# Side-by-side transfers in the ordering clock of a hybrid encoder-trunk kernel

## The chip, the cores and the metric

The kernel runs on one core of a Trainium2 chip. The metric is the device time of one execution in microseconds (us); several executions are timed, and one more is profiled.

## The reference

One layer of an encoder trunk on 2048 tokens of 1024 channels, all in float32. The part that matters here is branch C:

```python
h = rmsnorm(x, pre_g) * (1 + scale) + shift          # shift, scale, gate from silu(c) @ w_ada
q_lat, kv_lat, k_rope, gm_in, rw_in, z, g_logit = split_last(h @ w_in, IN_SPLITS)
y_mla = mla_mixer(...)      # attention of 8 heads, causal by chunks of 64
y_gm  = gmlp_mixer(...)     # gated mixing inside 128-token blocks
# branch C, rwkv7_mixer, 8 heads of 64, one step per token:
#   state = state * w_t + (state @ a_t) b_t^T + v_t k_t^T ;  y_t = state @ r_t
branches = stack([y_mla, y_gm, y_rw]) * silu(z)
merged = sum over branches of (branch @ w_br) * sigmoid(g_logit)
x = x + gate * rmsnorm(merged @ w_out, post_g)
```

## The kernel before, in words

**Stages.** The 2048 tokens are worked in four blocks of 512. For each block `s` there is a recurrence stage, `wkv(s)` (L969), and then an attention stage, `attention(s)` (L1334); the last block ends with `finish` (L1660). Every large product is made of three matmuls with 128x512 results (`mm3`, L595), since each operand is split into a high and a low part; they write the PSUM tiles `pd` and are called gemm matmuls below. Their weights (`wh`, `wl`) are loaded again for every use, by transfers that SP issues. Gemm work that nothing in a stage needs soon (gates, branch projections, the end of the block before) is the filler of that stage.

**A round of the recurrence.** Branch C is computed in chunks, two heads at a time, so a stage has four rounds and the kernel sixteen. A round goes through these steps:

- `prepare` (L1009): TensorE multiplies `ard` with `bk` (the `pst<-ard,bk` matmuls). ScalarE copies parts of the result to `abc`; VectorE makes the masked copies `ak` and `MB`.
- At the end of `prepare`, four transfers write quarters of `abc` side by side into the DRAM tile `md`, and four read `md` into quarters of `mb`.
- `inverses` (L1148): VectorE inverts small triangular matrices in 31 steps. They are 58 short instructions that write `X` and `tx`, each needing the one before. Then four transfers write `X` into quarters of the DRAM tile `xd`.
- `advance` (L1171): four transfers read `xd` into diagonal blocks of `xtb`. TensorE's first use of them are the `pss<-Pm,xtb` matmuls. Then follow `u`, `n`, `Wm`, `UV` and `QG`.
- `states` (L1236): eight small steps in turn on TensorE (`pss<-S,QG`) and VectorE (`S<-pss`), and the output `Y`.

**What sets the order.** The program is written by generators that take turns. A class `Pace` (from L99) keeps a clock for this. After each instruction is written, `note` (L154) puts down when it would end: it takes the latest of the times at which its inputs were written and its outputs last used (`wrote`, `used`, by tile name), finds a free slot on its engine, and adds a duration from a formula. For a transfer these are 0.45 us of the queue, 1.1 us, its bytes, and 0.8 us (`DLAT`). `ready` (L260) asks of each generator when the tiles of its next TensorE step would be there, and `run` (L291) lets the one go on that is ready first; filler goes where nothing else is ready.

TensorE runs its instructions in the order in which the program writes them (L331). The orders of VectorE, ScalarE, GpSimd and of SP's transfers are made by the framework's scheduler from the same program. On every engine, and on SP's queue, an instruction whose input isn't there holds up all that stand behind it. The clock itself isn't run on the chip: it decides orders alone.

Helpers issue every instruction through one traced call, so all rows of the profile carry its line, L123, and are told apart by their tiles.

Of the kernel before, what the change touches and what calls it, by code (L numbers as in the profile page):

```python
# [92 lines left out]
class Pace:  # L93
# [60 lines left out]
    def note(self, i):  # L154
        eng = str(i.engine).split(".")[-1]
        dma = "DMA" in type(i).__name__
        src, dst, n, full, f32 = [], [], 1, 0, False
        for l, aps in ((src, i.ins), (dst, i.outs)):
            for a in aps:
                ap = getattr(a, "bass_ap", None)  # L160
                if ap is None:
                    continue
                l.append(ap.tensor.name)
                m = 1
                for _, c in a.ap[1:]:
                    m *= c
                full += l is src and m > 1
                if dma:
                    m = 4 * m * a.ap[0][1]
                if eng != "PE" or l is dst:  # L170
                    n = max(n, m)
                elif a.dtype == F32:
                    f32 = True
        dep = 0.0
        for x in src:
            dep = max(dep, self.after(self.wrote.get(x), eng))
        for x in dst:
            for e in self.used.get(x, {}).items():
                dep = max(dep, self.after(e, eng))
        if eng == "PE":  # L180
            if f32 and not i.is_transpose:
                dur = 2 * max(.111, n * 2 / 2400)
            elif f32:
                dur = max(.108, n * 2 / 2400)
            else:
                dur = max(.061, n / 2400 + .0135)
            (r, c), (nr, nc) = i.tile_position, i.tile_size
            if dep <= self.t and all(r >= b or r + nr <= a for a, b in self.beside[1]):

                at = self.beside[0]  # L190
                self.beside[1].append((r, r + nr))
            else:
                at = max(self.t, dep)
                self.beside = at, [(r, r + nr)]
            t, p = max(self.t, at + dur), self.t
            self.pe += t - max(p, at)
            self.t = t
        elif dma:
            dur = n / 3.6e5
            t = self.slot("queue", max(dep, self.t - self.early), .45) + 1.1  # L200
            t = self.slot("DMA", t, dur) + dur + DLAT
            eng = "DMA"
        else:
            psum = any(x.startswith(("pd", "ps")) for x in src)
            op = type(i).__name__
            if eng == "Activation":
                f = str(i.func).split(".")[-1]
                if f in ("Exp", "Gelu", "Sin") and f != self.table or f == "Tanh" and self.table not in ("Exp", "Gelu"):
                    self.table = "Exp" if f == "Tanh" else f
                    t = self.slot(eng, max(dep, self.t - self.early), 1.28)  # L210
                dur = .08 + n * .00084 + .04 * (not psum) + .09 * (len(src) > 1) + .09 * (len(dst) > 1)
            elif eng == "DVE":
                dur = .065 + n / (960 if psum or full > 1 or n < 128 else 1920) + .065 * (full < len(src))
                if "Reciprocal" in op:
                    dur = .07 + n * .0063
                elif "Scan" in op or "Reduce" in op:
                    dur = n * (.0021 if "Scan" in op else .00118)
            else:
                dur = .12 + n * .00216 if n <= 512 else .55 + n * .0013
                if n <= 16 and "TensorTensor" in op:  # L220
                    dur = .3 + n * .165
            dur *= SLOW

            port = ("port",) if eng == "Pool" or eng == "DVE" and not psum else ()
            t = self.slot(eng, max(dep, self.t - self.early), dur, port) + dur
        for x in dst:
            self.wrote[x] = (eng, t)
        for x in src + dst:
            u = self.used.setdefault(x, {})
            u[eng] = max(u.get(eng, 0.0), t)  # L230
# [1539 lines left out]
```

## Time and profile before

| | us |
|---|---|
| median of 3 runs | 3145.57 |
| lowest and highest run | 3144.99, 3150.43 |
| the profiled execution | 3146.36 |
| its span, first to last instruction | 3144.4 |
| TensorE matmuls (PE), busy | 2927.0 |
| VectorE (DVE), busy | 1731.6 |
| ScalarE (ACT), busy | 1216.7 |
| GpSimd (POOL), busy | 621.5 |
| TensorE's mean granted clock, as a share of full speed | 0.964 |

The profiled execution takes 3146.36 us, 1.96 us more than its span. Busy times are sums over the span; PE is TensorE's matmuls, PEld its weight loads beside them, SPq the sequencer of SyncE that issues transfers. The clock is granted at one of two levels, 1.00 (2.4 GHz) or 0.50 (1.2 GHz). Moved bytes come to 654.17 MB, 208 GB/s on average.

### The profile page before, as it was taken

To read this page: it belongs to the slowest core of one execution; us is meant where nothing else is said; L and a number is where in the kernel's file an instruction comes from. 1 tells how busy PE (TensorE), PEld (TensorE's weight loads), DVE (VectorE), ACT (ScalarE), POOL (GpSimd) and SP (SyncE) were. 2 spreads that over 40 slices of the span, in tenths; PEclk is the share of its full clock that TensorE was granted. 3 is DMA by queue.
4 is the path that set the end of the run, shared out by engine and by line. 5 is a ranking of instruction groups with operands and counts; after the bars stand their busy time and mean duration, and the time that the engine had idled before them with its cause. 6 is when DMAs were issued, how large, how long until landed. Compare 5 with 4: busy or idle time off the path is not lost. (4 is left out here: it accounts for less than half of the span.)

```text
span 3144.4 us, 47954 instructions
## 1 busy us (share of the span) xinstructions
PE 2927.0 (93%) x16156; PEld 2391.6 (76%) x16156; DVE 1731.6 (55%) x4578; ACT 1216.7 (39%) x2806; POOL 621.5 (20%) x618
## 2 busy tenths in 40 slices
PE   5889998789999999999999998999999999999997
PEld 4667776668867787878877776887787777788876
DVE  6434767365366654466356664446645665566632
ACT  4324433353333424444232323544433232466621
POOL 2223232241022212122011101113201110222210
PEclk8999999879999999999999998999999999999998
DMA  8888855767566678765676577556558657744366
GB/s 273 271 271 264 251 182 182 242 210 229 200 210 223 192 226 265 225 196 166 211 251 199 166 230 231 185 177 209 155 169 250 198 171 230 224 137 128 113 207 204
DMA packets 524962, 654.17 MB, mean 208 GB/s; under 512 B 141648, under 2 KB 254380, under 8 KB 524716
## 3 DMA queue, kind: packets, MB, share of 16 engines
q1 hardware_dynamic: 524544, 651.06, 65.9%
q8 instruction: 128, 2.10, 0.3%
q14 instruction: 118, 0.97, 0.1%
q10 hardware_dynamic: 172, 0.05, 0.0%
HBM read 461.91 MB, written 189.01 MB: 207 GB/s over the span
## 5 line engine op out<-in xcount | busy, mean ns | idle before, releaser
L123 PE MATMUL pd<-hh,wh 128*128 128x512 f32 x1952 | 814.5, 417 | 19.3 <-ACT wh L123 10.3
L123 PE MATMUL pd<-hh,wl 128*128 128x512 f32 x1952 | 776.2, 398 | 6.1 <-DVE wl L123 4.3
L123 PE MATMUL pd<-hl,wh 128*128 128x512 f32 x1952 | 774.6, 397 | 2.5 <-DVE hl L123 1.5
L123 PEld LDWEIGHTS pd<-hh,wh 128*128 128x128 f32 x1952 | 374.5, 192 | 102.9 <-ACT wh L123 13.2
L123 PEld LDWEIGHTS pd<-hh,wl 128*128 128x128 f32 x1952 | 372.9, 191 | 94.7 <-DVE wl L123 8.3
L123 PEld LDWEIGHTS pd<-hl,wh 128*128 128x128 f32 x1952 | 374.8, 192 | 70.2 <-DVE hl L123 3.4
L123 DVE TENSOR_TENSOR pw<-pst,ph 128x512 fp32r<-128x512 f32 (+2 forms) x352 | 197.0, 568 | 255.2 <-ACT ph L123 253.6
L123 PE MATMUL pd<-brh,wh 128*128 128x512 f32 x576 | 252.0, 438 | 23.0 <-DVE gt L123 13.6
L123 ACT ACTIVATE ph<-pst 128x512 fp32r<-128x512 f32 (+2 forms) x352 | 171.7, 497 | 235.8 <-PE pst L123 197.8
L123 PE MATMUL pd<-brl,wh 128*128 128x512 f32 x576 | 232.4, 404 | 1.3 <-DVE brl L123 1.3
L123 PE MATMUL pd<-brh,wl 128*128 128x512 f32 x576 | 232.4, 403 | 0.0
L123 DVE TENSOR_SCALAR_CACHE_REDUCE p<-pss 128x512 f32<-128x512 f32 (+2 forms) x320 | 192.6, 607 | 62.6 <-PE pss L123 58.7
L123 ACT ACTIVATE p<-p,nm 128x512 f32<-128x512 f32 (+3 forms) x288 | 189.8, 661 | 79.1 <-DVE nm L123 78.9
L123 POOL TENSOR_TENSOR wl<-wr,wh 128x512 fp32r<-128x512 f32 x96 | 129.2, 1347 | 442.1 <-ACT wh L123 362.9
L123 ACT ACTIVATE wh<-wr 128x512 fp32r<-128x512 f32 x162 | 101.5, 628 | 220.0 <-PE pd L123 75.7
L123 PE MATMUL pst<-consts,p 128*128 128x128 f32 x1088 | 165.2, 277 | 7.9 <-DVE otm L123 3.1
L123 PEld LDWEIGHTS pd<-brh,wh 128*128 128x128 f32 x576 | 112.3, 195 | 58.6 <-DVE gt L123 11.6
L123 PE MATMUL pso<-ph,v 128*128 128x256 f32 x576 | 153.5, 287 | 2.4 <-ACT ph L123 2.3
L123 PE MATMUL pso<-pw,v 128*128 128x256 f32 x576 | 149.2, 286 | 6.3 <-DVE pw L123 6.0
L123 PEld LDWEIGHTS pst<-consts,p 128*128 128x128 f32 x1088 | 130.4, 143 | 24.7 <-issue 6.5
L123 PE MATMUL pss<-kh,qh 96*128 96x512 f32 (+2 forms) x320 | 131.1, 410 | 18.8 <-ACT kh L123 18.1
L123 POOL TENSOR_TENSOR kl<-stg,kh 96x512 fp32r<-96x512 f32 x80 | 103.8, 1300 | 223.8 <-ACT kh L123 194.6
(291 smaller groups left out, 4947.5 us busy)
## 6 DMA issues: line engine op xcount, KB each, us to landing
wh<-kept SPq DMA_DIRECT2D x486, 256.0 KB
wl<-kept SPq DMA_DIRECT2D x486, 256.0 KB
kept<-wh SPq DMA_DIRECT2D x162, 256.0 KB
kept<-wl SPq DMA_DIRECT2D x162, 256.0 KB
wr<-in_w_in SPq DMA_DIRECT2D x120, 256.0 KB
gate_d<-gt SPq DMA_DIRECT2D x64, 256.0 KB
part_d<-gt SPq DMA_DIRECT2D x64, 256.0 KB
p<-part_d SPq DMA_DIRECT2D x64, 256.0 KB
```

Source lines behind the costliest of these rows:

```text
L123: r = f(*a, **k)
```

## The change

The clock's rule for transfers is altered in two lines. Before, a transfer into a tile waited, in the clock, for every earlier use of that tile, earlier transfers into or out of it too; four transfers into quarters of one tile were timed one after the other. After, a transfer no longer waits in the clock for other transfers that use the tile it writes, and a tile counts as written when the latest of its transfers has landed. Nothing else is altered; no instruction, size or buffer is.

```diff
@@ -176,7 +176,8 @@
             dep = max(dep, self.after(self.wrote.get(x), eng))
         for x in dst:
             for e in self.used.get(x, {}).items():
-                dep = max(dep, self.after(e, eng))
+                if not (dma and e[0] == "DMA"):
+                    dep = max(dep, self.after(e, eng))
@@ -224,7 +225,8 @@
         for x in dst:
-            self.wrote[x] = (eng, t)
+
+            self.wrote[x] = (eng, max(t, self.wrote[x][1]) if dma and x in self.wrote else t)
```

The programs have the same 14129 matmuls and 2911 transfers, in other orders. Three places of the third recurrence stage, first round (chunks of block 2, heads 0 and 1), show what moved. A line of "..." stands where rows are left out.

TensorE at the first use of `xtb`, before: between the second half of the next round's `pst<-ard,bk` and `xtb` stand the rest of that round's `prepare` and 51 gemm matmuls.

```order
L123 MATMUL pst<-ard,bk 128x128 x8
L123 MATMUL pso<-vt,ak 64x64 x4
...
L123 MATMUL pst<-consts,bkb 128x128 x8
...
L123 MATMUL pst<-r,rkb 128x512
...
L123 MATMUL pss<-Pm,xtb 128x128 x8
L123 MATMUL pd<-hh,wh 128x512
L123 MATMUL pd<-hl,wh 128x512
L123 MATMUL pd<-hh,wl 128x512
```

The same place now:

```order
L123 MATMUL pst<-consts,sq 128x2 x4
L123 MATMUL pd<-brh,wh 128x512
L123 MATMUL pd<-brl,wh 128x512
L123 MATMUL pd<-brh,wl 128x512
...
L123 MATMUL pss<-Pm,xtb 128x128 x8
L123 MATMUL pst<-consts,sq 128x128 x4
L123 MATMUL pst<-consts,ard 128x128 x4
```

`xtb` is now used while the next round's `prepare` is still at its `sq` products, which stand on either side; its `ard,bk` and `bkb` matmuls follow later. Up to that round's second `pst<-lat,w2a` matmul the two orders are equal; from there to `sq` there are 24 gemm matmuls now, and were 12.

VectorE at the last steps of `inverses`, before (`ak` and `MB` are of the next round):

```order
L123 TENSOR_TENSOR ak<-pst,consts 128x256
L123 TENSOR_TENSOR tx<-X,mb 128x24
L123 TENSOR_TENSOR MB<-pst,consts 128x2x2x64
L123 TENSOR_TENSOR X<-X,tx 128x8x3
L123 TENSOR_TENSOR ak<-pst,consts 128x256
L123 TENSOR_TENSOR tx<-X,mb 128x16
L123 TENSOR_TENSOR MB<-pst,consts 128x2x128
L123 TENSOR_TENSOR X<-X,tx 128x8x2
L123 TENSOR_TENSOR tx<-X,mb 128x8
L123 TENSOR_TENSOR X<-X,tx 128x8
```

Now:

```order
L123 TENSOR_TENSOR tx<-X,mb 128x28
L123 TENSOR_TENSOR X<-X,tx 128x7x4
L123 TENSOR_TENSOR tx<-X,mb 128x24
L123 TENSOR_TENSOR X<-X,tx 128x8x3
L123 TENSOR_TENSOR tx<-X,mb 128x16
L123 TENSOR_TENSOR X<-X,tx 128x8x2
L123 TENSOR_TENSOR tx<-X,mb 128x8
L123 TENSOR_TENSOR X<-X,tx 128x8
```

The next round's masks no longer stand among these steps. Between the first and the last `X` of this round there were 29 other instructions, and there are 20 now.

SP's queue around the transfers of `X`, before:

```order
L123 DMA wl<-kept 128x512
L123 DMA xd<-X 256x1x32 x4
L123 DMA wh<-kept 128x512
L123 DMA gt<-gate_d_373 128x512
L123 DMA wl<-kept 128x512
L123 DMA xtb<-xd 32x8x32 x4
L123 DMA mg_d_352<-gt 128x512
```

Now:

```order
L123 DMA wh<-kept 128x512
L123 DMA gt<-gate_d_373 128x512
L123 DMA xd<-X 256x1x32 x4
L123 DMA xtb<-xd 32x8x32 x4
L123 DMA X<-in_consts 128x256
L123 DMA wl<-kept 128x512
```

The three loads that stood between `xd` and `xtb` stand elsewhere; the next weights follow `xtb`.

Counted on TensorE between the last `pst<-ard,bk` matmul of a round and its first `pss<-Pm,xtb` matmul, gemm matmuls and others (the latter in brackets):

| stage | before, rounds 1 to 4 | now, rounds 1 to 4 |
|---|---|---|
| 1 | 318 (80), 309 (111), 183 (132), 237 (97) | 216 (47), 138 (95), 114 (63), 126 (57) |
| 2 | 216 (80), 210 (107), 177 (139), 165 (125) | 129 (27), 126 (63), 141 (63), 141 (57) |
| 3 | 210 (80), 201 (103), 174 (106), 174 (129) | 120 (27), 132 (71), 108 (75), 126 (39) |
| 4 | 210 (80), 201 (103), 186 (105), 180 (129) | 120 (27), 132 (71), 108 (75), 126 (39) |

## Rows read from the trace of the kernel before

**Rows 1.** The page, part 1: busy us, share of the span, instructions of each engine.

```profile
PE 2927.0 (93%) x16156; PEld 2391.6 (76%) x16156; DVE 1731.6 (55%) x4578; ACT 1216.7 (39%) x2806; POOL 621.5 (20%) x618
```

**Rows 2.** TensorE's waits over the span: who waited for what, us, times, longest.

```profile
PE pss L123 <- DMA xtb<-xd: 2.0, 1, 2.0
```

**Rows 3.** TensorE in time, third stage, round 1: start, us, operation, count.

```profile
1607.08 1.16 PE L123 MATMUL pst<-ard,bk 64*128 64x128 f32 x16
...
1635.72 0.95 PE L123 MATMUL pst<-consts,sq 128*128 128x2 f32 x8
...
1670.67 1.95 PE L123 MATMUL pss<-Pm,xtb 128*128 128x128 f32 x16
```

**Rows 4.** VectorE in time, the same round: first and last `X`.

```profile
1628.03 0.25 DVE L123 SCALAR_TENSOR_TENSOR X<-mb,X 128x31 f32<-128x31 f32 x1
...
1654.80 0.17 DVE L123 TENSOR_TENSOR X<-X,tx 128x8 f32<-128x8 f32 x1
```

**Rows 5.** SP's queue in time, the same round: when its transfers were issued.

```profile
1655.00 2.57 SPq L123 DMA_DIRECT2D xd<-X  x4
...
1659.38 1.81 SPq L123 DMA_DIRECT2D xtb<-xd  x4
```

**Rows 6.** The chain that ended last: start, us, what.

```profile
2358.72 23.14 PE pd L123 x102
...
2451.26 4.01 DMA wl<-kept
...
2657.74 1.79 DMA xtb<-xd
```

**Rows 7.** One stretch of that round: us, then each engine's busy time (count).

```profile
1627.00:1656.00 29.00, 27.50 (x163) 21.43 (x161) 27.21 (x90) 7.20 (x15) 4.17 (x3) 1.00 0.72 236
```

**Rows 8.** The same stretch, VectorE's instructions on `X` and `tx` alone.

```profile
1627.00:1656.00 29.00, 14.80 (x58) 1.00 0.72 236
```

**Rows 9.** Twelve stretches, stages 1 to 3: last `ard,bk` to first `xtb` matmul.

```profile
283.50:377.50 94.00, 88.84 (x453) 68.79 (x452) 66.88 (x186) 43.18 (x86) 25.03 (x20) 0.98 0.83 248
337.40:432.90 95.50, 93.02 (x513) 74.26 (x513) 61.65 (x151) 38.77 (x73) 25.97 (x22) 1.00 0.84 252
442.30:520.50 78.20, 68.62 (x416) 54.00 (x417) 52.61 (x147) 27.92 (x66) 21.88 (x19) 0.96 0.50 152
503.70:580.90 77.20, 72.95 (x420) 59.04 (x420) 41.03 (x115) 22.84 (x48) 20.20 (x19) 1.00 0.72 226
885.40:958.30 72.90, 67.19 (x351) 52.08 (x350) 41.57 (x110) 22.04 (x54) 16.48 (x14) 0.93 0.71 216
943.30:1017.30 74.00, 71.22 (x410) 55.51 (x409) 49.04 (x139) 24.06 (x49) 15.08 (x14) 1.00 0.68 215
1028.80:1101.20 72.40, 66.03 (x416) 50.72 (x417) 45.77 (x138) 29.40 (x77) 16.73 (x16) 0.95 0.59 181
1094.70:1161.20 66.50, 63.15 (x376) 51.22 (x377) 38.81 (x119) 22.43 (x84) 11.15 (x12) 0.93 0.67 206
1608.20:1670.70 62.50, 61.01 (x345) 47.91 (x344) 38.67 (x111) 16.98 (x45) 7.86 (x7) 1.00 0.78 236
1655.80:1728.20 72.40, 68.95 (x396) 54.50 (x397) 46.15 (x134) 19.29 (x41) 8.70 (x9) 0.98 0.64 196
1745.50:1808.60 63.10, 59.75 (x347) 44.97 (x345) 39.70 (x123) 25.25 (x70) 10.16 (x11) 0.97 0.62 188
1800.30:1865.90 65.60, 62.55 (x390) 49.85 (x390) 39.52 (x121) 22.28 (x90) 7.52 (x9) 1.00 0.72 214
```

**Rows 10.** Two stretches where attention begins in stage 2; the granted clock is third from last.

```profile
1215.60:1220.60 5.00, 0.01 (x1) 0.01 (x1) 1.38 (x2) 2.96 (x6) 0.93 (x1) 1.00 0.76 179
1220.60:1227.40 6.80, 5.97 (x15) 4.50 (x16) 1.95 (x5) 2.88 (x6) 4.20 (x5) 0.50 0.64 206
```

**Rows 11.** Sum over 283:616, 885:1200, 1608:1914 and 2400:2700, the four recurrence stretches.

```profile
sum 1254.00, PE 1189.54 PEld 946.37 DVE 783.71 ACT 398.39 POOL 229.04; mean PE 297.38 PEld 236.59 DVE 195.93 ACT 99.60 POOL 57.26
```

## The prediction

> **What bounds the kernel now.** Read part 1 of the page first: TensorE's matmuls are busy for 2927.0 of 3144.4 us, VectorE for 1731.6 [rows 1]. So TensorE's own order, and what it waits for in that order, sets the time. The change alters no instruction, only orders, and the order of TensorE is the one that it alters directly. Next, TensorE's waits: of all its waits one single wait, of 2.0 us, was for `xtb` [rows 2]. In fifteen of sixteen rounds the inverted matrices were there before TensorE came to them. That cover is what the change takes away, so the question is how thick it was.
>
> Then one round in time. In stage 3, round 1, the last `ard,bk` matmul ends at 1607.08 + 1.16 = 1608.24, and TensorE comes to `xtb` at 1670.67 [rows 3]. In between, `X` runs on VectorE from 1628.03 to 1654.97 [rows 4], the four `xd` stores are issued from 1655.00 and the four `xtb` loads from 1659.38 to 1661.19 [rows 5]. A landing takes 1.79 us after the last issue, as the one `xtb` wait in the chain shows [rows 6]. So `xtb` lands at 1662.98. The **need** of this round is 1662.98 - 1608.24 = 54.7 us, TensorE gave it 62.4, and 7.7 us were to spare.
>
> Where do 54.7 us go? Transfers are the small part: from the last `X` to the landing it is 8.0 us for eight of them. In the stretch 1627 to 1656 VectorE is busy for 27.21 of 29.00 us [rows 7], and only 14.80 of that is `X` and `tx` [rows 8]. The other 32 instructions take 12.4 us, 0.39 each. The inversion shares VectorE with everything else.
>
> **The change, part by part.** Before, the clock timed four transfers into quarters of a tile in a row, which its own formula makes more than 2.35 us each; a round has four such groups, so some 25 us of its forecast were waiting that the queue doesn't do (rows 5 show four issued in 1.81 us). This error stood in for another: the clock fills gaps on VectorE freely, while the real engine runs its order. The change removes the first error and leaves the second.
>
> *TensorE comes earlier.* A gemm matmul costs 23.14 / 102 = 0.227 us [rows 6]. In stage 3, round 1, the order is unchanged up to the second `lat,w2a`; 12 more gemm matmuls then stand ahead of `sq`, which started at 1635.72 [rows 3]: 1635.72 + 2.7 + 0.95 for `sq` + 6 x 0.227 = 1640.7. That is 30 us sooner than 1670.67. Of these, 90 gemm matmuls (210 less 120) make 20.4 us, and 53 others 9.6, or 0.18 each. I use both prices for every round.
>
> *VectorE's share shrinks a little.* 20 instead of 29 other instructions lie between the first and last `X`: 9 x 0.39 = 3.5 us less. The need becomes 51.2 us, and `xtb` lands at 1659.4. TensorE is there at 1640.7 and waits **18.7 us**. Everything behind it on TensorE waits too, since no filler can overtake.
>
> *The other rounds.* Time left = stretch [rows 9] less moved work; wait = 51.2 less that. Stage 1: left 64.9, 53.8, 50.1, 44.8; waits 0, 0, 1.1, 6.4. Stage 2: 43.6, 47.0, 50.5, 48.8; waits 7.6, 4.2, 0.7, 2.4. Stage 3: 32.5, 51.0, 42.5, 38.5; waits 18.7, 0.2, 8.7, 12.7. Stage 4 now has stage 3's counts: again 40. Together 8 + 15 + 40 + 40 = **103 us**. If the 20 others were out of the way the need would be 43.4 and the sum 33; if as many stand there as in the fullest rounds before (some 31, 55.5 us) it is 165. I take 103, the round that I could follow row by row.
>
> *The clock.* Where TensorE stood idle for 5.00 us at the start of an attention stage, the granted clock was 0.50 in the 6.80 us after it, and matmuls ran at half speed there [rows 10]: up to 3.4 us lost. Eight of the waits above are over 5 us: 0 to 27 us, and I take half, 14, since after `xtb` come small steps that wait for VectorE anyway. The Trainium skill (TensorE: Matmul & The Clock Gate, HAM oscillation) says that a wait between groups of matmuls sends the clock down and the next group starts slow each time; by that rule it would be the full 27 and the time 3266. The trace agrees that it happens after 5 us.
>
> *SP's queue.* `xd` waits for `X`, and the weight loads behind it wait with it. The one such wait for weights in the chain is 4.01 us [rows 6]; eight rounds give 0 to 32 us. I take 0: there are three buffers of each weight part, and a TensorE that stands still doesn't empty them. GpSimd and ScalarE lose nothing that TensorE would wait for: they get the same instructions.
>
> *What comes back.* Filler that leaves the rounds runs later, after the last round or in attention; its 0.227 us stay. In the four recurrence stretches TensorE is idle for 1254.00 - 1189.54 = 64.5 us [rows 11]. Between 0 and 64.5 could be closed, when VectorE has caught up during a wait. Most of that idle time is hops inside the rounds that stay; I take 10.
>
> *Other tiles.* The rule also shortens, in the clock, pairs of loads for attention's keys and loads into a buffer whose store is still running. They gate one step of TensorE each and few of them; I price these at nothing, covered by the gemm filler around, with some us either way in the range.
>
> Sum: 103 + 14 + 0 - 10 = +107. The profiled execution took 3146.36 us (0.8 above the median of the runs), so **3253 us**.
>
> **The rivals.**
>
> *Faster.* The earlier rounds are real gains: `xtb` lands before TensorE comes, the stage's chain ends sooner, and half of the 64.5 idle us closes: 3146 - 32 = 3114. For it: transfers do run side by side [rows 5], so the clock is now truer. It decides where the need falls below the time left, which is 32.5 to 51 us in most rounds. Against it: `X` alone is 14.80 us, and 8.0 us of transfers follow it; first `X` came 19.8 us after `ard,bk`. That is 42.6 with VectorE quite free. The Trainium skill (Perfetto Trace Analysis, Identifying the Most-Contended Engine) calls matmul busy time a bad measure and weight-load time a better one; that is 76% here [rows 1], so by that rule TensorE has slack to take the waits in, and the time would be this rival's. The trace speaks against it: an idle stretch within TensorE's order isn't slack that a later matmul can fill. Chance 0.08.
>
> *No change.* The waits for `xtb` only take the place of waits that TensorE makes in the same stretches now: 3146. But those are 64.5 us in all against 103. Chance 0.04. That the change does nothing is excluded: the orders differ.
>
> *Worse.* Needs of 55.5 us and the full loss of clock: 165 + 27 = 192, 3338 us. For it: first `X` may now also stand behind the `S` steps of the round before, which TensorE paces. Chance 0.13.
>
> **How the numbers follow.** My forecast has 0.75, the worse case 0.13, so slower has 0.88; faster 0.08; same 0.04. A measurement of this kernel tells some 0.2%, 6 us, from no change. The range: sum at its low end 33 + 0 - 15 is 3165, which leaves out both rivals above (0.12) and little else; at the upper end 3340 takes in the worse case. 3165 to 3340.
>
> **What would show it.** In the changed profile, `PE pss <- DMA xtb<-xd` should lead TensorE's waits, with about a dozen waits and near 100 us, the longest of 15 to 20 at the first rounds of stages 3 and 4, and the recurrence stages of blocks 3 and 4 longer by some 40 us less what filler left them. `X` should again take 25 to 30 us from first to last. The granted clock should be below 0.964. If that wait stays below 20 us in total, the need was over-read and I am wrong; if the span grows without it, the time went to weights or attention.

## The result and the profile after

The changed kernel takes 3252.95 us (median of 4 runs, 3247.32 to 3253.4), the kernel before 3147.68 beside it. The ratio is 1.0332, with a 95% interval of 1.0315 to 1.0349: slower by 3.3%. TensorE's mean granted clock in the profiled execution is 0.949, against 0.964 before.

Part 1 of the page of the changed kernel: busy us, share of the span and instructions of each engine. Its span is 3251.6 us, 107.2 more than before.

```profile
PE 2932.1 (90%) x16156; PEld 2401.6 (74%) x16156; DVE 1716.8 (53%) x4575; ACT 1216.5 (37%) x2804; POOL 622.0 (19%) x621
```

Against [rows 1] TensorE's matmuls are busy for 5.1 us more, so nearly all of the 107.2 us is idle time of TensorE. Three instructions went over from VectorE to GpSimd; the rest differs in order alone. Its waits, in the view of [rows 2] (who waited for what, us, times, longest):

```profile
PE pss L123 <- DMA xtb<-xd: 107.8, 13, 12.7
PE pd L123 <- ACT brh L123: 32.2, 6, 11.3
PE pst L123 <- DVE yo L123: 14.0, 5, 4.7
PE pst L123 <- DMA wada<-in_w_ada: 13.0, 1, 13.0
...
PE pd L123 <- DMA wh<-kept: 1.3, 1, 1.3
PE pd L123 <- DMA wl<-kept: 0.8, 2, 0.4
```

The wait for `xtb` leads: 13 waits and 107.8 us, where there was one of 2.0. The second row has grown tenfold: the wait of the branch projections for `brh` was one of 2.8 us before. Waits for weights hardly exist.

```profile
PE pd L123 <- ACT brh L123: 2.8, 1, 2.8
```

Stage 3, round 1, as in [rows 3] to [rows 5]. TensorE in time: start, us, operation, count, and in brackets the idle time before it and what ended it.

```profile
1615.13 1.16 PE L123 MATMUL pst<-ard,bk 64*128 64x128 f32 x16
...
1648.54 0.40 PE L123 MATMUL pd<-brh,wl 128*128 128x512 f32 x1
1661.62 3.75 PE L123 MATMUL pss<-Pm,xtb 128*128 128x128 f32 x16 [12.69 <-DMA xtb<-xd]
...
1792.26 3.76 PE L123 MATMUL pss<-Pm,xtb 128*128 128x128 f32 x16 [5.59 <-DMA xtb<-xd]
```

The last `ard,bk` matmul ends at 1616.29, TensorE has nothing left at 1648.93 (1661.62 less 12.69), and `xtb` comes at 1661.62. Time left 32.6 us, need 45.3. The last row is round 3 of the same stage. VectorE and SP's queue in that first round:

```profile
1632.06 1.51 DVE L123 SCALAR_TENSOR_TENSOR X<-mb,X 128x31 f32<-128x31 f32 x9 [1.12 <-DMA mb<-md]
...
1654.00 0.17 DVE L123 TENSOR_TENSOR X<-X,tx 128x8 f32<-128x8 f32 x1
```

```profile
1654.20 2.56 SPq L123 DMA_DIRECT2D xd<-X  x4
...
1658.24 1.82 SPq L123 DMA_DIRECT2D xtb<-xd  x4
```

`X` runs for 22.1 us, from 1632.06 to 1654.17, and another 7.4 us pass until TensorE goes on. VectorE, all of it and its instructions on `X` and `tx` alone, in a view of stretches as in [rows 7] and [rows 8], the columns the same (one engine's time in the second row):

```profile
1632.10:1654.50 22.40, 16.84 (x77) 12.88 (x75) 19.31 (x78) 5.27 (x9) 1.76 (x2) 0.96 0.62 193
1632.10:1654.50 22.40, 12.95 (x58) 0.96 0.62 193
```

The 58 steps take 12.95 us and 20 other instructions 6.36.

### The profile page after: what moved, and what is told of

The parts are those of the page before. It is cut to its first block, busy times and chain, and to the rows that moved or that the text cites. A ratio compares the mean times of both kernels' runs of the same rounds, so it can differ in the third digit from the quotient of the medians.

```text
span 3251.6 us, 47897 instructions
## 1 busy us (share of the span) xinstructions
PE 2932.1 (90%) x16156; PEld 2401.6 (74%) x16156; DVE 1716.8 (53%) x4575; ACT 1216.5 (37%) x2804; POOL 622.0 (19%) x621
## 5 line engine op out<-in xcount | busy, mean ns | idle before, releaser
L123 PE MATMUL pss<-Pm,xtb 128*128 128x128 f32 x256 | 55.0, 402 | 107.8 <-DMA xtb<-xd 107.8
```

What stands on the lines that cost most here:

```text
L123: r = f(*a, **k)
```

## The experiments

The number to read them by is the **work** between a round's last `ard,bk` matmul and `xtb` on TensorE: its gemm matmuls there times 0.227 us, and the other matmuls there by their usual (median) durations in the trace before. It is an estimate from each kernel's order, a mean over sixteen rounds, good to about 1 us; single rounds differ by 20 us and more. The ratio is to the kernel before on the same chip, with its 95% interval; the wait is that of the profiled execution.

| kernel | work, us | wait for `xtb`, us | median, us | ratio |
|---|---|---|---|---|
| changed kernel | 37.7 | 107.8 | 3252.95 | 1.0332 (1.0315 to 1.0349) |
| recurrence tiles alone | 39.0 | 94.8 | 3236.87 | 1.0274 (1.0253 to 1.0295) |
| other formula for VectorE | 43.0 | 16.2 | 3165.94 | 1.0063 (1.0043 to 1.0083) |
| 6 us later | 45.1 | 27.5 | 3185.36 | 1.0118 (1.0095 to 1.0140) |
| `X` steps x 2 | 48.7 | 11.6 | 3164.01 | 1.0048 (1.0031 to 1.0065) |
| `X` steps x 3 | 50.9 | 6.4 | 3134.34 | 0.9948 (0.9931 to 0.9966) |
| 12 us later | 52.3 | 6.6 | 3149.60 | 1.0008 (0.9993 to 1.0023) |
| other formula, `X` steps x 2 | 54.8 | 9.8 | 3150.49 | 1.0017 (1.0002 to 1.0032) |
| `X` steps x 4 | 56.7 | 10.2 | 3144.00 | 0.9985 (0.9969 to 1.0002) |
| recurrence tiles in a row | 60.7 | 2.6 | 3151.23 | 1.0009 (0.9993 to 1.0024) |
| kernel before | 61.9 | 2.0 | 3147.68 | 1 |
| kernel before, `X` steps x 2 | 71.1 | 1.2 | 3179.39 | 1.0100 (1.0080 to 1.0119) |
| 24 us later | 71.6 | none | 3199.73 | 1.0155 (1.0137 to 1.0174) |

**Which tiles?** The theory: the loss is lost cover of `xtb`. The rival: other tiles, timed by the same rule, cost as much. First, the four groups of a round timed in a row again.

```diff
-                if not (dma and e[0] == "DMA"):
+                if not (dma and e[0] == "DMA") or x.split("_")[0] in ("md", "mb", "xd", "xtb"):
```

> The clock times the transfers into md, mb, xd and xtb in a row again, as the kernel before does; for all other tiles the changed rule stays. Theory (the lost cover of xtb is the whole loss): work on TensorE between a round's last ard,bk matmul and xtb is back at 46 to 86 us, so the xtb wait falls from 107.8 us to under 15 and the time is 3147, within 15. Rival (the rule costs through the other tiles, attention's loads above all): xtb waits vanish too, but the wait of pd for brh stays at 20 us or more and the time is over 3180. If the theory holds and brh stays, its 32 us were not paid in full.

Measured: 1.0009 (0.9993 to 1.0024), the `xtb` wait 2.6 us, the `brh` wait 1.5. The whole loss is gone, so other tiles by themselves cost nothing that can be measured. Then the reverse.

```diff
-                if not (dma and e[0] == "DMA"):
+                if not (dma and e[0] == "DMA" and x.split("_")[0] in ("md", "mb", "xd", "xtb")):
```

> The reverse: the changed rule for md, mb, xd and xtb alone, all other tiles timed in a row as before. Theory: work between ard,bk and xtb is 33 to 54 us as in the changed kernel, the xtb wait is 95 to 120 us and the time 3235 to 3260. Rival (other tiles): below 3200. The wait of pd for brh, 32.2 us in the changed kernel and 2.8 before, tells whose it is: near 3 if it belongs to the other tiles, near 30 if it comes from the rounds.

TensorE's waits in this run:

```profile
PE pss L123 <- DMA xtb<-xd: 94.8, 11, 14.0
PE pd L123 <- ACT brh L123: 31.3, 7, 9.4
```

Ratio 1.0274 (1.0253 to 1.0295): most of the loss comes from these four groups alone. The remaining 0.6% is clear of the intervals, so the other tiles do cost something once the rounds are short as well; the `xtb` wait is 13.0 us longer with them. The `brh` wait is there too, so it comes from the rounds, and not from another tile that the rule shortened. Of the two edited lines the first is the change: with the second by itself, TensorE's, VectorE's and SP's orders are those of the kernel before.

**What is the order worth without the wait?** TensorE's order is kept row for row, but the loads of `xtb` read a constant and no longer need `X`. This leaves the use of the inverted matrices out. The orders of the other engines and of SP's queue move with it: on VectorE 370 of 4575 instructions stand at another place.

```diff
+                pace.as_if = pace.name(xd)
                 for pb in range(4):
                     SY.dma_start(xtb[pb * 32:(pb + 1) * 32, :, pb * 32:(pb + 1) * 32],
-                                 xd[pb * 8:(pb + 1) * 8].rearrange("x a b -> a x b"))
+                                 io["consts"][0:32, C_X:C_N].rearrange("a (x b) -> a x b", b=32))
+                pace.as_if = None
```

> The changed kernel with TensorE's order kept row by row, but the four loads of xtb read a constant in place of xd, so that they wait for no X; in the clock they still count as reading xd. This leaves the use of the inverted matrices out; the inversion itself still runs. Theory (the order is good, only xtb is late): the 107.8 us of xtb waits go and nothing takes their place, time 3110 to 3150, which would also be what the earlier rounds are worth. Rival (other VectorE work was late as well and only hidden behind the wait): waits for ak, QG, UV, S or Y grow by over 40 us and the time stays over 3170. The wait of pd for brh stays near 30 us if it comes from the filler that left the rounds.

Measured: 1.0003 (0.9987 to 1.0018), 3152.66 us. Part 1 of its page, and then the waits of its TensorE:

```profile
PE 2910.3 (93%) x16156; PEld 2380.5 (76%) x16156; DVE 1715.7 (55%) x4575; ACT 1217.2 (39%) x2804; POOL 621.7 (20%) x621
```

```profile
PE pd L123 <- ACT brh L123: 30.3, 6, 11.3
PE pst L123 <- DVE yo L123: 13.5, 6, 4.7
...
PE pst L123 <- ACT sq L123: 11.9, 5, 5.3
...
PE pss L123 <- DVE lastp L123: 6.6, 1, 6.6
```

The time misses the expected 3110 to 3150 by 2.7 us, at its upper end. The run settles three things. Its span, 3142.9 us, is 108.7 shorter than the changed kernel's: 107.8 of waits and 21.8 of matmul time (2932.1 less 2910.3) go, and 20.9 of other idle time appears, for `sq` and `lastp` above all; how much of it the waits had covered, and how much the other engines' new orders brought, isn't separated. So the waits are the whole loss. Second, the order with `xtb` for nothing is as fast as the kernel before and not faster, so on balance the earlier rounds are worth nothing. Third, the `brh` wait is still 30.3 us. It belongs to the order and not to the `xtb` waits.

The 21.8 us are almost all in the matmuls right behind the wait, as the groups of instructions show (busy us, mean ns, idle time before). The changed kernel, then this run:

```profile
L123 PE MATMUL pss<-Pm,xtb 128*128 128x128 f32 x256 | 55.0, 402 | 107.8 <-DMA xtb<-xd 107.8
```

```profile
L123 PE MATMUL pss<-Pm,xtb 128*128 128x128 f32 x256 | 32.6, 282 | 0.0
```

**How much cover is right?** A constant is added to the clock's time for `xtb`, with the changed rule everywhere: 12, then 24, then 6 us. The diff of the first; the other two have their number in its place.

```diff
+            if dma and x.split("_")[0] == "xtb":
+                self.wrote[x] = (eng, max(self.wrote[x][1], t + 12.0))
```

> The changed rule everywhere, and in the clock xtb counts as written 12 us later than its formula says. Work between ard,bk and xtb becomes 43 to 67 us against a need of some 50. Theory (only the missing cover costs): the xtb wait falls to 10 to 40 us, the time to 3150 to 3185. Rival (shared queue or clock losses that the waits do not show): the wait falls but the time stays over 3210. Second rival (the earlier rounds are gains once xtb is there in time): under 3140.

Measured: 1.0008 (0.9993 to 1.0023), 3149.60 us, just under the expected range, the wait 6.6 us, below the 10 to 40 expected. Some 15 us of work given back, of the 24 that the change took, is enough.

```diff
+            if dma and x.split("_")[0] == "xtb":
+                self.wrote[x] = (eng, max(self.wrote[x][1], t + 24.0))
```

> As the run before with 24 us in place of 12: work between ard,bk and xtb is 55 to 82 us, over the need in every round, as much cover as before or more. Theory: no xtb wait over 2 us, brh wait as whatever the other tiles leave, time 3147 within 12. Rival (cover bought with filler is paid later, where filler is missing): over 3165, with idle time of TensorE in the attention stages or at the end grown by as much.

Measured: 1.0155 (1.0137 to 1.0174). The theory fell here and the rival held in its main point: too much cover costs as well. It isn't an `xtb` wait, of which there is none, but in part a small step behind it. The group for `UV` in the kernel before, in the changed kernel and in this run:

```profile
L123 PE MATMUL pss<-UV,MB 128*128 128x64 f32 x512 | 63.0, 281 | 5.7 <-DVE QG L123 5.7
```

```profile
L123 PE MATMUL pss<-UV,MB 128*128 128x64 f32 x512 | 59.7, 274 | 0.1
```

```profile
L123 PE MATMUL pss<-UV,MB 128*128 128x64 f32 x512 | 81.6, 331 | 21.4 <-DVE QG L123 21.4
```

This step takes 34.3 us more than in the kernel before, out of 54.0 us more span. The rival's idle time is the smaller part of it: TensorE's matmuls are busy for 38.2 us more (2965.2) and idle for 15.8 more, and the granted clock is 0.958. I read it so: the filler was used up ahead of `xtb`, and the hops behind it stand bare. That reading wasn't tried by itself, and the other 20 us are spread over many groups.

```diff
+            if dma and x.split("_")[0] == "xtb":
+                self.wrote[x] = (eng, max(self.wrote[x][1], t + 6.0))
```

> The changed rule with xtb 6 us later in the clock. Work between ard,bk and xtb becomes 38 to 61 us, mean 45 against 38 in the changed kernel and 52 with 12 us. Theory (each us of work put back takes one us of wait off in each of the 13 rounds that waited): xtb wait 40 to 65 us, time 3180 to 3205. Rival (a step: all or nothing): time within 15 of 3253 or within 10 of 3148.

Measured: 1.0118 (1.0095 to 1.0140), 3185.36 us, in the expected range for another reason. TensorE's waits in this run:

```profile
PE pd L123 <- ACT brh L123: 30.1, 5, 12.3
PE pss L123 <- DMA xtb<-xd: 27.5, 5, 9.1
PE pd L123 <- DVE gt L123: 15.3, 9, 4.6
PE pd L123 <- DVE lastp L123: 15.1, 3, 8.0
```

The `xtb` wait fell by 80.3 us, which is 6.2 in each of 13 rounds for 7.4 us more work: on average nearly one for one, as the theory has it; the 40 to 65 us that I expected from it were too many. Single rounds follow it less well: three still wait 7.2 to 9.1 us. The time didn't fall as far, since the projections' waits for `gt` and `lastp` came on top of that for `brh`.

What is the `brh` wait? In the changed kernel, at the start of the attention stage of block 2, TensorE's last gemm matmul starts at 1213.00, and it then stands for 11.30 us. SP's queue there:

```profile
1213.13 0.38 SPq L123 DMA_DIRECT2D wl<-kept  x1
1216.90 0.34 SPq L123 DMA_DIRECT2D out<-y  x1
1217.29 0.42 SPq L123 DMA_DIRECT2D yg_d<-ut  x1
...
1218.76 0.48 SPq L123 DMA_DIRECT2D yg<-yg_d  x1
```

And ScalarE, which makes `brh`:

```profile
1224.00 0.63 ACT L123 ACTIVATE brh<-yg 128x512 fp32r<-128x512 f32 x1 [9.98 <-DMA yg<-yg_d]
```

SP stands at `out<-y` from 1213.51 to 1216.90, with the store of `ut` behind it; then the store, the load `yg` and the cast follow one another until 1224.63. TensorE's filler is used up by then. With 12 us more cover this wait is 1.2 us, with `X` steps x 3 it is 1.6. So it goes with the cover, roughly: it is 30.1 at 45.1 us of work and 11.1 at 43.0, under the other formula. Which link of this chain is the late one wasn't tried.

**The clock's other error.** By the clock's formula a step of 60 elements takes 0.065 + 60/960 = 0.13 us on VectorE. The groups of the changed kernel:

```profile
L123 DVE TENSOR_TENSOR X<-X,tx 128x60 f32<-128x60 f32 x48 | 11.6, 242 | 1.2
L123 DVE TENSOR_TENSOR tx<-X,mb 128x60 f32<-128x60 f32 x48 | 11.3, 235 | 1.2
```

So the clock has the inversion at about half its price, besides filling gaps as it likes. The next runs mend the price instead of adding a constant; the filling of gaps is altered in none. First the `X` and `tx` steps doubled, under the changed rule.

```diff
             dur *= SLOW
+            if eng == "DVE" and dst[0].split("_")[0] in ("X", "tx"):
+                dur *= 2.0
```

> The changed rule everywhere, and the clock's duration of the X and tx steps on VectorE doubled, which brings their 58 steps to 14.9 us a round in the clock (7.5 before), near the 14.80 us that the trace showed. Work between ard,bk and xtb is 41 to 70 us, mean 49. Theory (the clock was wrong in this place, and a clock right in both places has no loss): xtb wait 15 to 50 us, time 3150 to 3185. Rival (a truer clock beats the old pair of errors): under 3140.

Measured: 1.0048 (1.0031 to 1.0065), 3164.01 us, as the theory expects; the wait of 11.6 us is below its 15 to 50, and the one for `brh` is 18.2. Then three times, which also stands for the other instructions among the steps.

```diff
+            if eng == "DVE" and dst[0].split("_")[0] in ("X", "tx"):
+                dur *= 3.0
```

> As the run before with the durations tripled, 22.4 us a round, which also stands for the other instructions that VectorE runs among the X steps. Work between ard,bk and xtb is 44 to 73 us, mean 52, fewer other instructions among the X steps (mean 17 in place of 18 in the changed kernel and 30 before). Theory: xtb wait under 25 us, time 3140 to 3165. Rival (truer clock beats the old pair of errors): under 3135 with the xtb wait under 10.

Measured: 0.9948 (0.9931 to 0.9966), 3134.34 us. The rival held: this version beats both kernels, the one before by 0.5%. Part 1 of its page, and its wait for `xtb`:

```profile
PE 2911.3 (93%) x16156; PEld 2384.9 (76%) x16156; DVE 1716.6 (55%) x4571; ACT 1219.3 (39%) x2808; POOL 626.8 (20%) x625
```

```profile
PE pss L123 <- DMA xtb<-xd: 6.4, 3, 2.6
```

Its span is 12.9 us shorter than that of the kernel before, and its matmuls are busy for 15.7 us less (2911.3 against 2927.0). So the gain lies in shorter matmul time and not in less waiting. But three times isn't the truer price: the steps were measured at about twice.

Four times, to see whether the gain was one lucky order:

```diff
+            if eng == "DVE" and dst[0].split("_")[0] in ("X", "tx"):
+                dur *= 4.0
```

> The changed rule with the X and tx steps four times as long in the clock, 29.9 us a round. Work between ard,bk and xtb is 48 to 73 us, mean 57, against a mean of 52 with three times and 49 with twice. Theory (the time falls until xtb is covered in every round and rises behind that, as with 12 and 24 us added): no xtb wait over 3 us, time 3130 to 3160, so that three times was near the best. Rival (the time of the run with three times, 3134, is an accident of one order): this one lies above 3160 although its cover lies between that of the runs with 12 and 24 us added.

Measured: 0.9985 (0.9969 to 1.0002), 3144.00 us, the longest `xtb` wait 5.0 and not under 3. The time lies in the expected range, so the bottom of the curve is near, but 10 us between neighbours is more than their cover explains.

Then VectorE's whole formula by what the rows show, without any extra for `X`.

```diff
-                dur = .065 + n / (960 if psum or full > 1 or n < 128 else 1920) + .065 * (full < len(src))
+                dur = .15 + n / 960
```

> The changed rule, and the clock's formula for VectorE replaced by 0.15 us plus the row's elements over 960, for all its instructions; by the rows of the changed kernel this fits most of them (64 elements 222 ns, 256 elements 419, 512 elements 686). Work between ard,bk and xtb is 37 to 55 us, mean 43, like with 6 us added. Theory (truer durations alone cure little, since the clock still fills VectorE's gaps in an order that the engine does not run): xtb wait 25 to 60 us, time 3165 to 3205. Rival (the durations were the second error): xtb wait under 15, time under 3150.

Measured: 1.0063 (1.0043 to 1.0083), 3165.94 us, the wait 16.2 in 8 parts. Between the two: truer durations take most of the wait and four fifths of the loss away, and 0.6% stays. And with the `X` steps doubled on top:

```diff
-                dur = .065 + n / (960 if psum or full > 1 or n < 128 else 1920) + .065 * (full < len(src))
+                dur = .15 + n / 960
             dur *= SLOW
+            if eng == "DVE" and dst[0].split("_")[0] in ("X", "tx"):
+                dur *= 2.0
```

> As the run before, with the X and tx steps doubled on top. Work between ard,bk and xtb is 46 to 71 us, mean 55. Theory (it is the cover of xtb that decides, best just over the need of some 50): xtb wait under 12 us, time 3120 to 3150. Rival (the whole formula shifts other places for the worse or the better): under 3115 or over 3160 with the same xtb wait.

Measured: 1.0017 (1.0002 to 1.0032), 3150.49 us, just over the expected range, the wait 9.8. The cover is 4 us above that of the best version, the time 0.7% worse. Last, the kernel before with the `X` steps doubled, the price mended and the transfers still timed in a row.

```diff
             dur *= SLOW
+            if eng == "DVE" and dst[0].split("_")[0] in ("X", "tx"):
+                dur *= 2.0
```

> The kernel before, where transfers are timed in a row, with the X and tx steps doubled: the second error cured without the first. Work between ard,bk and xtb is 51 to 96 us, mean 72, against a mean of 61 in the kernel before and 74 with 24 us added. Theory (too much cover costs as well: filler used in the rounds is missing behind them): no xtb wait, waits of the UV step for QG over 12 us, time 3165 to 3205. Rival (a truer clock is better wherever it is truer): at or under 3148.

Measured: 1.0100 (1.0080 to 1.0119), 3179.39 us. As the theory has it, mending either error alone makes the kernel slower. The place is another than expected: `UV` waits 6.9 us for `QG` and not over 12, and the loss is spread (matmuls busy for 23.3 us more, idle for 14.0 more). Where it sits stays open.

## Why the prediction was right

The forecast was 3253 and the time is 3252.95. The mechanism held: lost cover of `xtb`, by the two runs on which tiles and the one with `xtb` for nothing. That the number fits to the microsecond is luck: the waits came out 4.8 us above their term, the clock 7.8 above, and what comes back 12.4 below, and these cancel.

*TensorE comes earlier.* In stage 3, round 1, forecast and trace agree: 32.5 us left against 32.6. Over all rounds the forecast's mean was 45.8; the trace gives 44.1 (the start of `xtb` less its wait). So the prices of 0.227 and 0.18 us place TensorE well on the mean; single rounds are off by up to 6.6 us (stage 1, round 3: 50.1 forecast, 43.5 measured).

*The need.* The forecast was 51.2 us everywhere. In the 13 rounds that waited it is 43.3 to 54.1, mean 49.5. In the round that I followed it is 45.3 and not 51.2: the first `X` comes 15.8 us after `ard,bk` in place of 19.8 [rows 3, 4], the run of `X` takes 22.1 in place of 23.4, the end 7.4 in place of 8.0. The step that failed is taking the old first `X` as given. In the kernel before, VectorE had two steps for `r` just ahead of it, and waited 4.35 us for the first of them:

```profile
1627.23 0.75 DVE L123 SCALAR_TENSOR_TENSOR r<-pd,vcol,xa 128x511 f32<-128x511 f32 x1 [4.35 <-ACT xa L123]
1627.90 0.21 DVE L123 SCALAR_TENSOR_TENSOR r<-lastp,vcol,xa 128x1 f32<-128x1 f32 x1
```

In the changed kernel the first of these comes at 1635.29, among the `X` steps, and the first `X` waits for `mb` alone, 1.12 us. VectorE's steps between `ard,bk` and these are the same in both traces.

*The waits by stage.* Forecast 8, 15, 40 and 40 us; measured 15.1, 25.7, 33.5 and 33.5. The sum is 107.8 against 103, the longest 12.7 and not 18.7. Two errors offset each other here. With the time left as measured and 51.2 us of need everywhere the waits would be 13, 25, 46 and 46, in all 130: TensorE came sooner than forecast, and that is nearly all that stages 1 and 2 lacked. In stages 3 and 4 needs below 51.2 took more than that off again. The sizes were off, the mechanism was right; "about a dozen waits near 100 us" held, "15 to 20" did not.

*Other signs.* The granted clock fell below 0.964, as said, to 0.949. The run of `X` was to take 25 to 30 us; it takes 18.6 to 29.0 over the sixteen rounds, and a need of 51.2 already held 23.4. Stages 3 and 4 were to be longer by 40 us less what filler left them; from the first `lat,w2a` matmul to the last `S` they are 21.0 and 15.0 us shorter, so the filler that left outweighs the waits.

*The clock.* Forecast 14 us, which is 1.75 for each of eight waits; with and without the waits in the same TensorE order it is 21.8, or 1.68 for each of thirteen. So the number of waits was short, and the price of one was right by luck: the reason given for halving it (small steps follow that wait for VectorE anyway) was wrong, since the 16 `xtb` matmuls come first and pay themselves, 3.75 us in place of 1.95 [rows 3]. The Trainium skill (TensorE: Matmul & The Clock Gate, HAM oscillation) has each group behind a wait start slow, and the forecast by that rule was 27, at 3.4 a wait. The trace agrees that each of the 13 groups started slow, at half that price. Against the kernel before, matmuls are busy for only 5.1 us more, because the new order without those waits keeps them busy for 16.7 less (2910.3 against 2927.0).

*SP's queue* as weights: forecast 0, measured 2.1 us. Right. But the queue stands behind `out<-y` in the longer wait for `brh`, which I had not named: 29.4 us more than before.

*Other tiles*: priced at nothing, and the run with the recurrence tiles in a row shows 1.0009. On top of shorter rounds they cost some 0.6%, which lies inside the waits above.

*What comes back*: forecast 10 us. Without `xtb` waits the new order is within 0.2% of the old one, so on balance nothing comes back from the earlier rounds; what filled the sum instead is the 20.9 us of other idle time by which the run without `xtb` waits has more. In all: 107.8 + 21.8 - 20.9, and -1.5 of the order, make 107.2.

*The rivals.* "Faster" fell: even with `xtb` there at once the kernel is not faster. The Trainium skill's preference for weight-load time (Perfetto Trace Analysis, Identifying the Most-Contended Engine) stood beside it, read as slack of 24% (100 less the 76% of [rows 1]). The Trainium skill says so of how close a kernel comes to its roofline, which isn't whether a wait can be filled. 107.8 us of waits moved the time by 107.2, so these found no slack. "No change" fell with it. "Worse" needed 55.5 us of need, and 49.5 was measured.

The first error did stand in for something: undone alone it cost 3.3%, the `X` price mended alone cost 1.0%, and both together, with the price as measured, 0.5%. Only at three times the formula, more than the steps take, is there a clear gain, of 0.5%. The second error that the prediction named, a clock that fills VectorE's gaps freely, was altered in no run; its share stays open.

## What to carry to other kernels

A planner's wrong cost may be the cover of something else: before it is corrected, read from the trace how long the resource that it delays is really needed, and how much TensorE work stands in between. Here the time over that work is, roughly, a bowl, with its bottom where the cover reaches the need or a little more (51 to 62 us of work against 49.5), and both sides cost: some 3% at 38 us, 1 to 1.5% at 71. Mend the durations that stand in a chain together with the rule: the rule alone lost 3.3%, with durations near the measured ones 0.5 to 0.6%. And measure neighbours of the best setting, since orders of nearly equal cover differ by up to 0.7%; what makes one of them better than the next stays open.

## What the runs showed of the hardware

A short wait costs more than its own length, since the matmuls behind it start slow. A stretch in which TensorE stands for `xtb`, and the one behind it, at the end of stage 2 and in stage 3; the granted clock is third from last:

```profile
1114.70:1117.80 3.10, 0.01 (x1) 0.00 (x0) 0.69 (x1) 0.63 (x1) 1.26 (x1) 0.83 1.04 293
1117.80:1121.70 3.90, 3.83 (x17) 3.87 (x18) 0.73 (x2) 0.00 (x0) 0.00 (x0) 0.50 0.97 301
...
1648.90:1661.60 12.70, 0.04 (x1) 0.01 (x1) 4.88 (x20) 0.82 (x2) 0.89 (x1) 0.65 0.25 57
1661.60:1666.30 4.70, 4.67 (x22) 4.70 (x23) 1.41 (x3) 0.00 (x0) 0.00 (x0) 0.50 0.04 13
```

After 3.1 us of standing the next 3.9 us had a granted clock of 0.50 (1.2 GHz), as 4.7 us had after 12.7. The 16 `xtb` matmuls took 3.75 us behind the wait of 3.16 us just as behind that of 12.69, and 1.95 without one in the kernel before; over 13 waits the slow starts made 21.8.

The larger part of a small VectorE step doesn't go with its elements: in the changed kernel most `X` and `tx` steps of 60 elements took 0.20 to 0.22 us, most of those of 8 elements 0.17. The means above are higher (235 to 242 ns) because a few steps took far longer: 38 of the 928 `X` and `tx` steps took over 0.4 us, up to 1.3. By the trace 92 of the 928 ran while a GpSimd instruction was at work, and all 38 are among them.
